# Channel shuffle on one core: three in-place slots of 68 KB in place of two input and three output buffers of 38 KB

## The chip, the cores and the metric

The kernel runs on one core of a Trainium2 chip. The metric is the device time of one execution in microseconds; the kernel before takes 316.18 us (median of 3 runs, 316.15 to 316.26). The profile comes from one execution and counts from its first instruction to its last.

## What is computed

The input is `[16, 64, 64, 256]` in fp32: 65,536 rows of 256 channels, 1 KB a row, 67.11 MB in all. In each row the 256 channels are read as 8 groups of 32 and written as 32 groups of 8:

```python
x = x.reshape(batch, h, w, groups, channels_per_group)   # 8 x 32
x = x.transpose(0, 1, 2, 4, 3)
x = x.reshape(batch, h, w, c)
```

There is no arithmetic. Every byte is loaded once and stored once, and each row is permuted inside itself.

## The kernel before, in words

A tile of q is q rows of 1 KB on each of the 128 partitions, so 128 q rows that lie together in HBM, q KB without a break for each partition. The list `_SLOTS` (line 12) cuts the 512 rows a partition into slots of one or two tiles: `[4, 8]`, `[28]`, twelve of `[38]`, and `[16]`, which makes sixteen tiles. The loop at line 45 goes over the slots. For each it takes an `in_tile` from a pool with two buffers and an `out_tile` from a pool with three (lines 36, 37, 46, 47), each buffer with room for 38 KB a partition, 190 KB a partition together.

For each tile three instructions are written down:

- line 55: SP issues the load, one DMA from HBM into the input buffer;
- line 57: VectorE (DVE) copies the tile from the input to the output buffer and permutes each row on the way, with a read pattern of step 32 inside the row and a dense write;
- line 61: ACT issues the store, one DMA from the output buffer to HBM.

`tc.manual_schedule` (line 43) keeps this order on each engine; the framework adds the waits. A load into an input buffer waits until the copy that read this buffer two slots earlier is done. A copy waits for its load and, through the output buffer, for the store of three slots earlier. A store waits for its copy. All loads go through SP's queue (q1 in the profile), all stores through ACT's (q10), each in order; the same 16 DMA engines serve both. PE and GpSimd do no work on the data.

Of the kernel before, what the change touches and what calls it, by code (L numbers as in the profile page):

```python
# [1 line left out]

# [4 lines left out]


F32 = mybir.dt.float32
P = 128  # L10

_SLOTS = [[4, 8], [28]] + [[38]] * 12 + [[16]]
_IN_BUFS = 2
_OUT_BUFS = 3


@with_exitstack
def kernel(
    ctx: ExitStack,
    tc: tile.TileContext,  # L20
    x: bass.AP,
    groups: bass.AP,
    out: bass.AP,
):
    nc = tc.nc
    b, h, w, c = x.shape
    G = int(groups)
    CPG = c // G
    assert G * CPG == c
    assert sum(map(sum, _SLOTS)) * P == b * h * w  # L30
    biggest = max(map(sum, _SLOTS))

    x_flat = x.rearrange("b h w c -> (b h w c)")
    out_flat = out.rearrange("b h w c -> (b h w c)")

    in_pool = ctx.enter_context(tc.tile_pool(name="in_pool", bufs=_IN_BUFS))
    out_pool = ctx.enter_context(tc.tile_pool(name="out_pool", bufs=_OUT_BUFS))

    def rows(flat, first, q):

        return flat[first * c : (first + P * q) * c].rearrange("(p f) -> p f", p=P)

    ctx.enter_context(tc.manual_schedule(engines=None))
    first = 0
    for parts in _SLOTS:
        in_tile = in_pool.tile([P, biggest * c], F32, name="in_tile")
        out_tile = out_pool.tile([P, biggest * c], F32, name="out_tile")
        at = 0
        pieces = []
        for q in parts:  # L50
            pieces.append((q, first, slice(at * c, (at + q) * c)))
            first += P * q
            at += q
        for q, start, cols in pieces:
            nc.sync.dma_start(out=in_tile[:, cols], in_=rows(x_flat, start, q))  # L55
        for q, start, cols in pieces:
            nc.vector.tensor_copy(  # L57
                out=out_tile[:, cols].rearrange("p (i j g) -> p i j g", j=CPG, g=G),
                in_=in_tile[:, cols].rearrange("p (i g j) -> p i j g", g=G, j=CPG),
            )  # L60
            nc.scalar.dma_start(
                out=rows(out_flat, start, q), in_=out_tile[:, cols]
            )


# [1 line left out]
_INS = ['x', 'groups']  # L67
_OUTS = [((16, 64, 64, 256), 'float32')]

_NUMBERS = {'groups': 8}  # L70


# [26 lines left out]
```

## Time and profile before

| | value |
|---|---|
| median of the runs | 316.18 us |
| span of the profiled execution | 314.4 us |
| what lies around the span (median less span) | 1.8 us |
| VectorE busy, 16 copies | 119.0 us, 38% of the span |
| loads, 16 DMAs | 67.11 MB |
| stores, 16 DMAs | 67.11 MB |
| median time from issue to landing, 38-KB tile | load 37.0 us, store 42.6 us |

The profiled execution's own time outside its span is not recorded; the table takes the median in its place, so that a change of the span is carried over to the time as it is.

How to read the page: part 2 cuts the span into 40 equal slices. The digits behind an engine are its busy share in tenths, those behind DMA the mean busy share of the 16 DMA engines, and GB/s is what they moved. A packet is booked in the slice in which it starts, so a single slice can lie above or below the true rate, and so can a short window. Part 3 gives the two queues with packets, bytes, and the share of the 16 engines' span that their packets took. A row of a tile on one partition goes as one packet here: 16 DMAs of 128 partitions and 16 closing packets of 4 B for each DMA are the 2,304 packets of a queue.

The trace also holds each DMA packet with its queue, size, start and duration. These are called the packet records below.

### The profile page before, as it was taken

How to read it: one execution, taken by the hardware profiler on the slowest of the kernel's cores; microseconds unless marked ns; L12 is line 12 of the kernel's file. 1: busy time of each engine (PE TensorE's matmuls, PEld its weight loads, DVE VectorE, ACT ScalarE, POOL GpSimd, SP SyncE). 2: the span in 40 equal slices, each digit the busy share in tenths (PEclk: the TensorE clock that was granted, in tenths of full speed). 3: DMA queues.
4: the chain of work that ended last, by engine and by line, in shares of the span. 5: the costliest groups of instructions: out<-in, count | busy, mean ns of one | idle time of the engine just before them, and what ended most of it. 6: DMA issues, size and time to landing. Idle time of an engine off the chain costs nothing.

```text
span 314.4 us, 132 instructions
## 1 busy us (share of the span) xinstructions
DVE 119.0 (38%) x16; POOL 0.2 (0%) x4
## 2 busy tenths in 40 slices
DVE  2081907309109109019028028037046055065400
POOL 0000000000000000000000000000000000000000
DMA  7999999999999999999999999999999999999997
GB/s 317 405 441 416 435 416 483 401 465 406 450 421 446 426 436 436 401 470 396 475 396 475 396 470 401 470 401 470 401 450 421 446 426 436 436 417 450 429 421 321
DMA packets 4608, 134.22 MB, mean 427 GB/s; under 512 B 512, under 2 KB 512, under 8 KB 768
## 3 DMA queue, kind: packets, MB, share of 16 engines
q1 hardware_dynamic: 2304, 67.11, 49.8%
q10 hardware_dynamic: 2304, 67.11, 49.4%
HBM read 67.11 MB, written 67.11 MB: 427 GB/s over the span
## 4 chain that ended last, share of the span: by engine, by line
DMA 76%; DVE 19%; issue 0%; SPq 0%; DVEq 0%
DMA in_tile<-in_x_dram 76%; DVE out_tile L57 19%; SPq L55 0%; DVEq L57 0%
## 5 line engine op out<-in xcount | busy, mean ns | idle before, releaser
L57 DVE COPY out_tile<-in_tile 128x9728 f32<-128x9728 f32 (+4 forms) x16 | 119.0, 7440 | 179.4 <-DMA in_tile<-in_x_dram 179.4
L80 POOL MEMSET const-uint8-127<- 128x1 uint8 x1 | 0.1, 103 | 0.0
L80 POOL MEMSET const-bfloat16-1.0<- 128x1 bf16 x1 | 0.1, 102 | 0.0
L80 POOL MEMSET const-float32-1.0<- 128x1 f32 x1 | 0.1, 100 | 0.0
L80 POOL MEMSET const-float32-0.0<- 128x1 f32 x1 | 0.1, 99 | 0.2 <-issue 0.2
## 6 DMA issues: line engine op xcount, KB each, us to landing
in_tile<-in_x_dram SPq DMA_DIRECT2D x12, 4864.0 KB, 37.0
out_dram<-out_tile ACTq DMA_DIRECT2D x12, 4864.0 KB, 42.6
in_tile<-in_x_dram SPq DMA_DIRECT2D x1, 3584.0 KB, 14.7
out_dram<-out_tile ACTq DMA_DIRECT2D x1, 3584.0 KB, 30.9
in_tile<-in_x_dram SPq DMA_DIRECT2D x1, 2048.0 KB, 30.4
out_dram<-out_tile ACTq DMA_DIRECT2D x1, 2048.0 KB, 15.2
in_tile<-in_x_dram SPq DMA_DIRECT2D x1, 1024.0 KB, 5.4
out_dram<-out_tile ACTq DMA_DIRECT2D x1, 1024.0 KB, 25.0
```

What stands on the lines that cost most here:

```text
L57: nc.vector.tensor_copy(out=out_tile[:, cols].rearrange("p (i j g) -> p i j g", j=CPG, g=G), in_=in_tile[:, cols].rearrange("p (i g j) -> ...
L80: nc = _bacc.Bacc("TRN2", target_bir_lowering=False, num_devices=1)
```

## The change

The two pools become one pool of three slots, each with room for 68 KB a partition (56 of the largest tile and 12 of `_SHIFT`), 204 KB together. The tiles are `[4, 8, 28]` in the first slot, then eight of `[56]`, then `[24]`: twelve tiles for sixteen.

A tile is loaded 12 KB further up in its slot than it is stored from. VectorE moves it down in place, in chunks of at most 12 rows: chunk by chunk, `src` is 12 KB above `dst`, so a chunk's source and destination touch but don't overlap, and each chunk is written where the one before it was read. A tile of 56 takes five copies (four of 12 rows, one of 8), one of 28 three, one of 24 two. The store of a tile still comes after all of its copies. A load into a slot now has to wait until the store that read this slot three slots earlier has landed, since the load writes over the bytes that it reads.

```diff
-_SLOTS = [[4, 8], [28]] + [[38]] * 12 + [[16]]
-_IN_BUFS = 2
-_OUT_BUFS = 3
+_SLOTS = [[4, 8, 28], [56]] + [[56]] * 7 + [[24]]
+_BUFS = 3
+_SHIFT = 12
...
-    biggest = max(map(sum, _SLOTS))
+    room = max(map(sum, _SLOTS)) + _SHIFT
...
-    in_pool = ctx.enter_context(tc.tile_pool(name="in_pool", bufs=_IN_BUFS))
-    out_pool = ctx.enter_context(tc.tile_pool(name="out_pool", bufs=_OUT_BUFS))
+    pool = ctx.enter_context(tc.tile_pool(name="pool", bufs=_BUFS))
...
-        in_tile = in_pool.tile([P, biggest * c], F32, name="in_tile")
-        out_tile = out_pool.tile([P, biggest * c], F32, name="out_tile")
+        slot = pool.tile([P, room * c], F32, name="slot")
...
-        for q, start, cols in pieces:
-            nc.sync.dma_start(out=in_tile[:, cols], in_=rows(x_flat, start, q))
-        for q, start, cols in pieces:
-            nc.vector.tensor_copy(
-                out=out_tile[:, cols].rearrange("p (i j g) -> p i j g", j=CPG, g=G),
-                in_=in_tile[:, cols].rearrange("p (i g j) -> p i j g", g=G, j=CPG),
+        for q, start, at in pieces:
+            nc.sync.dma_start(
+                out=slot[:, (at + _SHIFT) * c : (at + _SHIFT + q) * c],
+                in_=rows(x_flat, start, q),
             )
+        for q, start, at in pieces:
+            for lo in range(at, at + q, _SHIFT):
+                n = min(_SHIFT, at + q - lo)
+                src = slot[:, (lo + _SHIFT) * c : (lo + _SHIFT + n) * c]
+                dst = slot[:, lo * c : (lo + n) * c]
+                nc.vector.tensor_copy(
+                    out=dst.rearrange("p (i j g) -> p i j g", j=CPG, g=G),
+                    in_=src.rearrange("p (i g j) -> p i j g", g=G, j=CPG),
+                )
             nc.scalar.dma_start(
-                out=rows(out_flat, start, q), in_=out_tile[:, cols]
+                out=rows(out_flat, start, q), in_=slot[:, at * c : (at + q) * c]
             )
```

More of the change, by code (lines that the diff above doesn't have):

```diff
@@ L50 @@
         for q in parts:
-            pieces.append((q, first, slice(at * c, (at + q) * c)))
+            pieces.append((q, first, at))
             first += P * q
             at += q
-        for q, start, cols in pieces:
-            nc.sync.dma_start(out=in_tile[:, cols], in_=rows(x_flat, start, q))
-        for q, start, cols in pieces:
-            nc.vector.tensor_copy(
-                out=out_tile[:, cols].rearrange("p (i j g) -> p i j g", j=CPG, g=G),
-                in_=in_tile[:, cols].rearrange("p (i g j) -> p i j g", g=G, j=CPG),
-            )
+        for q, start, at in pieces:
+            nc.sync.dma_start(
+                out=slot[:, (at + _SHIFT) * c : (at + _SHIFT + q) * c],
+                in_=rows(x_flat, start, q),
+            )
+        for q, start, at in pieces:
[7 more added lines that the diff above has]
+                )
             nc.scalar.dma_start(
-                out=rows(out_flat, start, q), in_=out_tile[:, cols]
+                out=rows(out_flat, start, q), in_=slot[:, at * c : (at + q) * c]
             )
```

## The prediction

> **What bounds the kernel now.** I read the page first, parts 2 and 3:
>
> ```profile
> span 314.4 us, 132 instructions
> ...
> DMA  7999999999999999999999999999999999999997
> ...
> q1 hardware_dynamic: 2304, 67.11, 49.8%
> q10 hardware_dynamic: 2304, 67.11, 49.4%
> ```
>
> The two queues together fill the 16 DMA engines for 99.2% of the span, and only the first and last slice show a 7. The loads' packets took 0.4% of the span, 1.3 us, more than the stores' for the same bytes and count. Next the windows, one row for the middle (length, DVE busy, POOL busy, clock, DMA share, GB/s):
>
> ```profile
> 60.00:260.00 200.00, 75.15 (x9) 0.00 (x0) 1.00 1.00 433
> ```
>
> DMA share is 1.00. VectorE is busy for 75 of these 200 us. Part 4 gives it a share of the chain all the same:
>
> ```profile
> DMA 76%; DVE 19%; issue 0%; SPq 0%; DVEq 0%
> ```
>
> This is how the load of two tiles later is released (buffer free when the copy ends), not a limit: the DMA engines work on the other queue meanwhile. The timeline shows the beat:
>
> ```profile
> 71.31 8.75 DVE L57 COPY out_tile<-in_tile 128x9728 f32<-128x9728 f32 x1 [13.40 <-DMA in_tile<-in_x_dram]
> ...
> 94.33 8.77 DVE L57 COPY out_tile<-in_tile 128x9728 f32<-128x9728 f32 x1 [14.27 <-DMA in_tile<-in_x_dram]
> ...
> 278.19 8.73 DVE L57 COPY out_tile<-in_tile 128x9728 f32<-128x9728 f32 x1 [14.21 <-DMA in_tile<-in_x_dram]
> ```
>
> From 71.31 to 278.19 are nine beats, 22.99 us each, in which 38 rows go in and 38 out, and in each VectorE waits 14 us for a load. So the time is the DMA engines' work, and a gain can only come from what they do besides moving bytes.
>
> The packet records say how much that is. In the full stream, start to start on one engine, a packet of 4, 8, 16, 28 and 38 KB takes 0.1554, 0.3060, 0.6070, 1.0585 and 1.4353 us: 37.65 ns per KB and 4.7 ns per packet. A closing packet takes 5.9 ns. Check: a beat is 16 x 1.4353 + 2 x 0.006 = 22.98 us. One engine's 8,192 KB then cost 308.4 us, its 256 data packets 1.2 us, its 32 closing packets 0.2 us. The rest of the span is 1.75 us until the first packet, about 1.2 us after the last, and some 1.7 us ahead of 36 us and in the engines' uneven end. The records put 1.13 us of that on loads that take longer than their size asks, all before 36 us, when loads run nearly alone; behind it, no load does. Within rounding, this is the 1.3 us of part 3.
>
> **The change, part by part.**
>
> *Fewer, longer packets.* 24 DMAs for 32, 8 packets of each on an engine: 64 data packets less, 64 x 4.7 ns = 0.30 us, and 8 closing packets less, 0.05 us. Gain 0.35 us. A packet of 56 KB is not in the trace; by the two nearest rows (28 and 38 KB) it takes 56 x 0.03765 + 0.0047 = 2.113 us. Bounds: as above, or 1% longer, as loads ran around 20 us (third part).
>
> [...]
>
> *The in-place copies.* From the groups by form:
>
> ```profile
> L57 DVE COPY out_tile<-in_tile 128x4096 f32<-128x4096 f32 x1 | 3.9, 3873 | 7.6 <-DMA in_tile<-in_x_dram 7.6
> L57 DVE COPY out_tile<-in_tile 128x2048 f32<-128x2048 f32 x1 | 2.0, 2019 | 1.5 <-DMA in_tile<-in_x_dram 1.5
> L57 DVE COPY out_tile<-in_tile 128x1024 f32<-128x1024 f32 x1 | 1.1, 1092 | 4.1 <-DMA in_tile<-in_x_dram 4.1
> ```
>
> A chunk of 12 rows (3,072 elements) lies midway between 2,019 and 3,873 ns: 2.95 us. A tile of 56: 4 x 2.95 + 2.02 = 13.8 us, with about 0.05 us between copies 14.05 us. VectorE's sum grows from 119.0 to 1.09 + 2.02 + 6.98 + 8 x 13.8 + 5.9 = 126 us, far below the span. Whether a copy inside one slot runs at the pace of one between two buffers is not shown; between that pace and twice as long, I take the former, since elements, pattern and types are those of the rows above. The cost is nothing while it is hidden by the DMA queues; the cover is counted below.
>
> [...]
>
> *The load's new wait.* Load i+3 waits for store i to land, not for a copy. Behind it on SP stand only later loads. The records show how the queues share: packet by packet in turn, whatever the packets' sizes. So by hand:
> - Up to 15.8 us nothing differs (loads 4, 8, 28). Load 1 (56) then runs against two 4-KB and five 8-KB store packets and ends at about 34.6. Load 2 runs against two of 8 KB and five of 28 KB: 8 x 2.113 + 0.6 + 5.3, ends at about 57. Three more 28-KB packets: store 28 is through at about 61.
> - Load 3 now issues at 61.4 (a landing is seen 0.4 to 0.7 us after its last packet). Its packets enter 1.0 us later (before: issue 0.73, first packet 1.75) behind two or three store packets already taken (before: first store issued at 5.19, first packet at 9.2, two loads ahead). So near 67 us. Meanwhile store 1, issued at 34.6 + 0.6 + 14.05 = 49.3, fills the engines alone; stores alone run at full pace at the end of before. Cost 0.
> - Then pairs of 2 x 2.113: a load or store takes 33.8 us. Store 1 ends at 67 + 5 x 4.226 = 88.1, load 3 at 98.7, and so on: the slot for the next load is free some 10 us before it is its turn. Copy: when load n lands, store n-1 has about six of eight packets left, at pair pace over 20 us, against 0.6 + 14.05 + 1.4.
> - The tightest place is the end. The last packet of load 8 passes at 67 + 6 x 33.8 - 2.1 = 267.7. Six packets of store 7 (12.7 us) and load 9's eight of 24 KB (7.3 us) remain: work until 287.7. Store 8 can begin at 267.7 + 0.6 + 14.05 + 1.4 = 283.8. Slack 3.9 us. Then stores 8 and 9 run alone, as 38 and 16 do before. Cost 0.
>
> *The start.* Beyond 15.8 us the records hold 0.54 us of slow loads before: 0.18 spread over the first 38-KB load (1.3% of 13.6 us), and 0.36 in one packet on each engine at 32.9 us, for which I see no reason. After, loads run nearly alone until 43.8. At 1.3% (the 38-KB load, the nearest row) that is 0.36 us, at 3% (the 28-KB load, 0.26 of 8.5 us) 0.84. With or without the 0.36: 0 to 1.2 us in place of 0.54, so -0.54 to +0.66. By the nearest row it is 0.36 or 0.72; I take the middle: no change.
>
> *Sum*: 314.4 - 0.35 = 314.05 us of span; with 1.8 us around it (median less span) 315.83 us, 0.11% below the median. Its own range, by the start: 315.3 to 316.5.
>
> **The rivals.**
> 1. *The start goes well or the middle gains more*: the 0.36 and half of the spread vanish, or longer packets also hide other gaps: 315.0 to 315.5. For: the 0.36 came once only. Against: loads run alone for longer.
> 2. *Long rows slow the loads* (the other side). If 56-KB loads run 1.3% long not only at the start but beside stores too, 64 packets of 2.113 us cost 1.8 us more: 317.6 us. It decides from 0.7% (0.98 us: the 0.35 gained and 0.63 to the edge). For: the only packets that ran long are loads. Against: from 36 us on none did, at 38 and 16 KB.
> 3. *In-place copies are slow.* At 1.28 times the slack of 3.9 us is gone; at twice, 14 - 3.9 = 10 us idle before store 8: 326 us. For: such a copy is not in the trace. Against: the forms between two buffers lie close to one line from 4 to 38 rows.
> 4. *The change doesn't do what it says*: a 56-KB row goes as two packets. Then 64 + 64 more packets: 0.6 us on the forecast, 316.4, no difference.
>
> **How the numbers follow.** A measurement of this kernel can tell about 0.2%, 0.63 us, from no change, so the edges are 315.55 and 316.81. Main case 0.64, of which 0.21 falls below 315.55; rival 1, 0.09; rival 2, 0.15; rival 3, 0.08; rival 4, 0.04. Faster 0.21 + 0.09 = 0.30; same 0.43 + 0.04 = 0.47; slower 0.15 + 0.08 = 0.23. The range 315.0 to 317.2 leaves out rival 3 and two thirds of rival 2, 0.18.
>
> **What would show it.** Right: packets 2 x 1,728, DMA share 1.00 in the middle, VectorE near 126 us, copies of 3,072 elements near 2.95 us, landings 33.8 us apart, both queues' shares closer than 0.4%. Wrong: a slice below 9 near 61 or 285 us; a load queue's share above the store queue's by more than 0.6%; copies above 3.7 us; packets above 1,728 a queue.

## The result and the profile after

| | before | after |
|---|---|---|
| median (range, runs) | 316.17 us (316.15 to 316.26) | 317.89 us (317.50 to 318.38, 4) |
| span of the profiled execution | 314.4 us | 315.6 us |
| end of an engine's last packet, mean of the 16 engines | 312.97 us | 312.90 us |
| the same: first, median, last of the 16 engines | 312.86, 312.92, 313.28 us | 312.47, 312.75, 314.50 us |

The changed kernel is slower: 1.72 us, ratio 1.0056 [1.0042, 1.0070]. The forecast was 315.8 us, the range ended at 317.2. The profiled execution of the changed kernel took 317.50 us, the lower end of its times, so its trace shows 1.2 of the 1.72 us. All ratios here leave out executions that took over 1.5% longer than the fastest of their kernel, two of no_copy_56_3_slots and three of after_half_loads.

The lines of the page that answer to those of before:

```profile
span 315.6 us, 145 instructions
...
DVE 126.6 (40%) x47; POOL 0.2 (0%) x4
...
DMA  8999999999989999998999899989999998999986
...
DMA packets 3457, 134.22 MB, mean 425 GB/s; under 512 B 385, under 2 KB 385, under 8 KB 641
...
q1 hardware_dynamic: 1728, 67.11, 49.6%
q10 hardware_dynamic: 1728, 67.11, 49.1%
...
DMA 81%; DVE 13%; issue 0%; SPq 0%; DVEq 0%
```

The packets are the 1,728 of a queue that were foretold; the odd one, 3,457, is a packet of 24 B in the instruction queue at 0.2 us. Both queues' shares are lower; they stand 0.5 apart, between the 0.4 that the prediction set for right and the 0.6 for wrong. Scattered 8s are mostly booking: a 56-KB packet of 2.1 us counts in the slice where it starts, and none of them stands at 61 or 285 us, where the prediction looked for one. The middle by the windows (length, DVE busy, POOL busy, clock, DMA share, GB/s) is as full as before, and so is the rate, 435 GB/s for 433:

```profile
60.00:260.00 200.00, 82.86 (x30) 0.00 (x0) 1.00 1.00 435
```

The timeline shows the start of each tile's copies, and in the brackets how long VectorE had waited for the load:

```profile
59.84 13.96 DVE L64 COPY slot<-slot 128x3072 f32<-128x3072 f32 x5 [10.28 <-DMA slot<-in_x_dram]
99.86 14.01 DVE L64 COPY slot<-slot 128x3072 f32<-128x3072 f32 x5 [26.07 <-DMA slot<-in_x_dram]
133.74 13.96 DVE L64 COPY slot<-slot 128x3072 f32<-128x3072 f32 x5 [19.87 <-DMA slot<-in_x_dram]
...
269.54 13.93 DVE L64 COPY slot<-slot 128x3072 f32<-128x3072 f32 x5 [20.09 <-DMA slot<-in_x_dram]
294.15 5.91 DVE L64 COPY slot<-slot 128x3072 f32<-128x3072 f32 x2 [10.68 <-DMA slot<-in_x_dram]
```

Landings stand 33.9 us apart, a tile's copies take 14.0 us, and the last big tile's store is issued at 283.5 us: the beat, the copies and the cover at the end are those of the prediction.

So no average shows the loss. It is in the last microseconds, after (first fence) and before (second fence):

```profile
312.00:313.00 1.00, 0.00 (x0) 0.00 (x0) 1.00 0.29 123
313.00:314.00 1.00, 0.00 (x0) 0.00 (x0) 1.00 0.06 25
```

```profile
312.00:313.00 1.00, 0.00 (x0) 0.00 (x0) 1.00 0.65 279
313.00:314.00 1.00, 0.00 (x0) 0.00 (x0) 1.00 0.00 0
```

A DMA share of 0.06 is one engine of sixteen. Before, most engines are busy past 312 us and all stop together. After, most have stopped by then and one works on, to 314.50 us. The mean engine ends 0.07 us earlier, the median engine 0.17 us earlier, and the last one 1.22 us later: that is the growth of the span.

**Where the late engine lost it.** The packet records don't name the engine. I put a packet down to the engine whose packet before it ended as it began, which fits to a few ns behind 60 us. They give each packet's duration, and that of nearly all goes by the size alone: a typical 56-KB packet takes 2.113 us start to start, which is what 28 and 38 KB led to. Call a packet stalled when it takes over 15 ns more than its size asks. After 60 us, 1 of 1,328 load packets is stalled before (0.07 us in all), and 23 of 896 after (4.29 us, 0.02 to 0.50 us each). Stores hardly stall (2 of 1,168 after, 0.43 us). The late engine lost 1.64 us: seven of the stalled loads (1.21 us) and both stalled stores. Before, no engine is more than 0.36 us behind the median; after, the last one is 1.75 us behind it and 0.85 us behind the next. The whole time is set by that engine.

The late engine is also out of step with the others. Load 3 was issued at 62.0 us into an empty load queue. From 63.9 to 67.4 us 15 engines start their third 56-KB packet of store 1, and one, the late one, its first of load 3:

```profile
q10 hardware_dynamic: 15, 0.86, 56.7%
q1 hardware_dynamic: 1, 0.06, 3.8%
```

From then on it often loads while the others store. Between 60 and 260 us it moves data in the same direction as most engines in 52% of the time, each of the 15 others in 93% or more. Below, an engine is called out of step when this share is about a half or less.

### The profile page after: what moved, and what is told of

Same layout as the page of the kernel before. It is cut to its first block, busy times and chain, and to the rows that moved or that the text cites. A ratio compares the mean times of both kernels' runs of the same rounds, so it can differ in the third digit from the quotient of the medians.

```text
span 315.6 us, 145 instructions
## 1 busy us (share of the span) xinstructions
DVE 126.6 (40%) x47; POOL 0.2 (0%) x4
## 2 busy tenths in 40 slices
DMA packets 3457, 134.22 MB, mean 425 GB/s; under 512 B 385, under 2 KB 385, under 8 KB 641
## 3 DMA queue, kind: packets, MB, share of 16 engines
q1 hardware_dynamic: 1728, 67.11, 49.6%
q10 hardware_dynamic: 1728, 67.11, 49.1%
## 4 chain that ended last, share of the span: by engine, by line
DMA 81%; DVE 13%; issue 0%; SPq 0%; DVEq 0%
DMA out_dram<-slot 43%; DMA slot<-in_x_dram 39%; DVE slot L64 13%; SPq L55 0%; DVEq L64 0%
## 5 line engine op out<-in xcount | busy, mean ns | idle before, releaser
L64 DVE COPY slot<-slot 128x3072 f32<-128x3072 f32 (+2 forms) x47 | 126.6, 2694 | 173.4 <-DMA slot<-in_x_dram 172.2
## 6 DMA issues: line engine op xcount, KB each, us to landing
out_dram<-slot ACTq DMA_DIRECT2D x1, 3072.0 KB, 14.8
```

The source lines that it names most:

```text
L64: nc.vector.tensor_copy(out=dst.rearrange("p (i j g) -> p i j g", j=CPG, g=G), in_=src.rearrange("p (i g j) -> p i j g", g=G, j=CPG),)
```

## The experiments

Three things changed at once: rows of 56 KB for 38, copies inside a slot for copies between buffers, and loads that wait for a store to land. My theories of the stalls, by the names that the expectations use: SIZE, that long packets bring them; PLACE, that in-place copies do, by work on the memory beside the DMA engines; STEP, that the load queue runs dry once, near 61 us, and leaves engines out of step, which collect delays; LATE, that a load issued only a few packets ahead of its turn is served unevenly. PITCH (that rows 56 KB apart in HBM collide) and FETCH (the instruction packet) came up on the way. Each ratio is against the kernel before, run in the same batch, whose medians lay between 316.06 and 316.19 us.

**1. The changed kernel again**, with no edit.

> The changed kernel once more, unaltered, for its spread and for a second look at the packets. Three theories. STEP: the load queue runs dry once, from about 59 to 67 us, the 16 DMA engines take up load 3 at different packets, and an engine that is a packet out of step with the others collects delays; then the late engine shows again (some engine over 1 us behind the middle one at the end), and the time is 317.5 to 318.4. SIZE: packets of 56 KB make loads run long now and then beside stores; same time, but the late packets are spread over engines that are in step too. PLACE: copies inside the slot disturb the DMA to the same slot; same time, late packets fall in the copies' 14 us.

Measured: 318.89 us (316.69 to 320.72, 6 runs), 1.0084 [1.0052, 1.0115]. The profiled execution has 33 stalled loads (8.46 us). Its last engine ends at 315.46 us, 2.6 behind the median:

```profile
313.00:314.00 1.00, 0.00 (x0) 0.00 (x0) 1.00 0.17 74
314.00:315.00 1.00, 0.00 (x0) 0.00 (x0) 1.00 0.11 49
```

What follows: the loss is real, its size differs from run to run by 4 us, and again a few engines are late at the end. Here all 16 engines left the dry queue in step, so being out of step from there isn't needed for the loss.

**2 and 3. The tiles of before in the slots of after, and a start without the dry queue.**

```diff
-_SLOTS = [[4, 8, 28], [56]] + [[56]] * 7 + [[24]]
+_SLOTS = [[4, 8], [28]] + [[38]] * 12 + [[16]]        # same_tiles_3_slots
+_SLOTS = [[4], [36]] + [[56]] * 8 + [[24]]            # one_tile_head
```

> In place with three slots, but with the tiles of the kernel before (4 and 8, 28, twelve of 38, 16). STEP: by the queues' turns load 3 issues only after the 8 KB store, near 30 us, where load 2 has just ended: dry for a few us, so late engines are possible: 316.2 to 317.5. SIZE: no packet above 38 KB, so 316.2 within 0.3. PLACE: as the changed kernel, 317 or more.

> The changed kernel with the head 4, 36 in slots of their own in place of 4, 8, 28 in one slot; the eight tiles of 56 and the 24 stay. By the queues' turns load 3 issues at about 24 us and load 2 runs until 35, so the load queue never runs dry. STEP: no engine falls out of step, 315.8 (eight packets and a DMA fewer for each queue than the changed kernel, so down to 315.7). SIZE: 317.2 or more. PLACE: 317.2 or more.

Measured: 317.13 us (316.82 to 321.39, 12 runs), 1.0052 [1.0025, 1.0079]; and 318.88 us (317.94 to 319.19, 5), 1.0077 [1.0065, 1.0089]. The second has load 3 issued in time and is as slow as any: its stalls are 37 (6.43 us), and it is late at the end as well:

```profile
313.00:314.00 1.00, 0.00 (x0) 0.00 (x0) 1.00 0.35 147
314.00:315.00 1.00, 0.00 (x0) 0.00 (x0) 1.00 0.17 74
```

What follows: the dry queue near 61 us isn't needed. Being out of step is not ruled out, though: in one_tile_head five engines are out of step (35 to 49%, the others 87% or more), all 37 stalled loads are theirs, and they are the last five to end (314.46 to 315.49 us, the next at 313.39). The first run, in which one engine also lost 0.84 us to the instruction packet of experiment 4, says that 38-KB tiles don't cure it all, and raised PLACE and LATE.

**4 and 8. A fourth slot at 38 KB, then chunks of 13 rows.** With four slots the loads are issued some 18 us ahead of their turn (before: 14.8); the copies stay in place.

```diff
-_SLOTS = [[4, 8, 28], [56]] + [[56]] * 7 + [[24]]
-_BUFS = 3
+_SLOTS = [[4, 8], [28]] + [[38]] * 12 + [[16]]
+_BUFS = 4
```

In same_tiles_4_slots_13, `_SHIFT = 13` besides: 43 copies for 55.

> In place with four slots of 50 KB and the tiles of the kernel before. Loads issue about 20 us ahead of their turn, the queue never runs dry. STEP: 316.2 within 0.3, no late engine. SIZE: 316.2 within 0.3. PLACE: 317 or more, since the copies are in place here as well.

> In place with the permutation, tiles of the kernel before, four slots of 51 KB and a shift of 13 in place of 12: a tile of 38 takes three copies in place of four, 42 copies in place of 53. With a shift of 12 the one late engine of this kernel lost 0.84 us beside an 8 KB packet of the instruction queue at 268.7 us. FETCH (that packet is the cause): it falls out of the run, no engine is late, 316.2 within 0.2 in place of 316.7. PLACE (copies in the slot cost DMA time): stays at 316.7.

Measured: 316.70 us (316.65 to 316.83, 11 runs), 1.0014 [1.0005, 1.0023]; and 316.35 us (316.17 to 316.62, 11), 1.0003 [0.9995, 1.0012]. The profile of the first names what remains, in part 3:

```profile
span 314.9 us, 169 instructions
...
q14 instruction: 2, 0.01, 0.0%
```

One of these packets, 8 KB of instructions, comes at 268.66 us. On the engine that takes it there is a gap of 0.30 us and then the only stalled load of the run, 0.54 us: that engine is 0.84 us late. With 157 instructions in place of 169 no such packet comes between 268 and 292 us, and the run is like before: 0 stalls, last engine at 313.23 us.

What follows: PLACE falls, as in-place copies of 38-KB tiles cost nothing (1.0003 in same_tiles_4_slots_13); FETCH holds, and is worth about 0.35 us here (316.70 less 316.35). In the changed kernel (145 instructions) the packet came after the end, at 316.83 us, so FETCH is not its cause.

**5, 6 and 7. No copies at all.** The copy loop (from line 60) is taken out and `_SHIFT` is 0, so the permutation is left out and a slot is only loaded and stored.

```diff
+_SLOTS = [[8]] + [[56]] * 9            # no_copy_56_3_slots
+_SLOTS = [[8], [45]] + [[51]] * 9      # no_copy_51_3_slots; no_copy_51_4_slots with _BUFS = 4
```

> Leaves the permutation out: each tile is stored from where it was loaded, so VectorE does nothing and the slots need no 12 KB more. Tiles 8 and nine of 56, three slots of 56. By the queues' turns a load issues some five packets (about 10 us) ahead of its turn, against two to four in the changed kernel. From the packet count alone (96 data and 12 closing packets fewer on an engine) 315.65 us. PLACE (copies disturb the DMA): 315.6, no stalled packet after 60 us. SIZE (56 KB packets stall): over 316.5, stalled load packets as before. LATE (a load issued only a few packets ahead of its turn stalls engines): between the two.

> Permutation left out, tiles 8, 45 and nine of 51, three slots. A load issues about five packets ahead. From the packet count 315.75 us. LATE: stalls, 316.3 or more, and more than with four slots. SIZE: stalls, the same as with four slots. PLACE: none.

> The same with four slots: a load issues about thirteen packets (27 us) ahead of its turn. LATE: 315.75 us and no stalled packet. SIZE: the same stalls as with three slots. PLACE: none in either.

Measured: 317.94 us (316.66 to 322.2, 11 runs), 1.0051 [1.0030, 1.0072]; 317.32 us (316.75 to 317.86, 9), 1.0031 [1.0017, 1.0044]; 317.02 us (316.50 to 317.37, 11), 1.0024 [1.0015, 1.0033]. Stalled loads are 17, 9 and 6. The first packet of a load waits about 28, 23 and 55 us in its queue: these loads are issued long before their turn.

What follows: without VectorE and with loads issued early, rows of 51 and 56 KB still cost 0.24 to 0.51%. That speaks for SIZE, and against PLACE and LATE as conditions of it. It doesn't speak for SIZE alone: in no_copy_56_3_slots four engines are out of step (32 to 42%), all 17 stalled loads are theirs, and they end last.

**11, 13 and 14. Long rows with the buffers of before.** Two input and two output buffers, one copy per tile, as in the kernel before but for the tiles (and a third output buffer less, to make room).

```diff
-_OUT_BUFS = 3
+_OUT_BUFS = 2
 _SLOTS = [[4, 8], [28]] + [[38]] * 12 + [[16]]    # out_of_place_38, as before
+_SLOTS = [[4, 8], [28]] + [[44]] * 10 + [[32]]    # out_of_place_44
+_SLOTS = [[4, 8], [28]] + [[50]] * 9 + [[22]]     # out_of_place_50
```

> The kernel before with two output buffers and its own tiles. Loads issue about three packets of 38 KB ahead, in place of five. SIZE: 316.2 within 0.2, no stalled packet. LATE: 316.6 or more, stalls on the packets behind a change of DMA.

> The same with ten tiles of 44 and one of 32: the step between 38 (no stalled packet, 316.12 us) and 50. By the packet count 0.15 us less than before, 315.95. SIZE: between, 315.9 to 316.5; if it is a limit between 38 and 50 KB, either no stalled packet or as many as at 50.

> The kernel before with two output buffers and tiles 4 and 8, 28, nine of 50, 22, all even, since copies of an odd number of rows took twice as long (51 rows 22.3 us) and spoiled the run with 51. Out of place, one copy a tile, no dry queue by the turns, about 75 us of slack a tile less the copy of 11.5 us. By the packet count 0.24 us less than before: 315.9. SIZE (load packets of 50 KB stall now and then whatever the rest of the kernel): stalled packets after 60 us, 316.5 to 317.2. STEP or in place alone: none, 315.9.

Measured:

| rows | us (range, runs) | ratio | stalled loads after 60 us |
|---|---|---|---|
| 38 KB | 316.12 (316.01 to 316.44, 11) | 1.0001 [0.9992, 1.0010] | 0 of 1,328 |
| 44 KB | 316.35 (316.13 to 317.05, 11) | 1.0012 [1.0003, 1.0021] | 3 of 1,104, 0.10 us |
| 50 KB | 317.52 (316.24 to 318.06, 6) | 1.0040 [1.0027, 1.0054] | 13 of 992, 2.29 us |

The middle of the 38-KB and of the 50-KB kernel by the windows:

```profile
60.00:260.00 200.00, 73.56 (x9) 0.00 (x0) 1.00 1.00 433
```

```profile
60.00:260.00 200.00, 80.67 (x7) 0.00 (x0) 1.00 1.00 433
```

Both are full. The 50-KB profile fell on that kernel's fastest execution (316.24 us; the other five took 317.36 or more), so its stalls are seen in a run where they did not add up on one engine. In it no engine is out of step (84% or more): long load packets stall in step too.

What follows: this is the cleanest answer. Same copies, same kind of buffers, 30% longer rows: 1.4 us (317.52 less 316.12). SIZE is shown, as a cost in time and in stalls; that the stalls make up the whole 1.4 us is not, since no slow execution was traced. LATE falls as the cause here: at 38 KB a load is issued 9.1 us before its first packet and nothing is lost, at 50 KB 12.2 us before, and it stalls. At shorter leads (6 to 7 us in the changed kernel, 7 to 8 in three slots at 38 KB) it is not ruled out.

**10. Rows of 51 KB with the buffers of before**, meant for the same question.

```diff
-_OUT_BUFS = 3
+_OUT_BUFS = 2
+_SLOTS = [[4, 8], [28]] + [[51]] * 9 + [[13]]
```

> The kernel before with two output buffers in place of three and tiles 4 and 8, 28, nine of 51, 13: out of place, one copy a tile. By the packet count 0.24 us less than before, 315.9. With two output buffers a copy waits for the store two slots earlier, so that a load issues some three packets ahead of its turn, as in the changed kernel. SIZE: stalled packets after 60 us, 316.6 to 317.3. LATE: the same. PLACE or the in-place slots: 315.9.

Measured: 366.2 us (363.81 to 367.05, 5 runs), 1.1582 [1.1557, 1.1608]. The copies got in the way, but they are not all. By groups (busy us, mean ns of one), this kernel and then the one with 50 rows:

```profile
L57 DVE COPY out_tile<-in_tile 128x13056 f32<-128x13056 f32 x9 | 200.4, 22274 | 116.9 <-DMA out_dram<-out_tile 116.9
```

```profile
L57 DVE COPY out_tile<-in_tile 128x12800 f32<-128x12800 f32 x9 | 103.5, 11500 | 156.6 <-DMA out_dram<-out_tile 156.6
```

One row more, an odd number, and a copy takes 22.27 us for 11.50: half the pace on VectorE. But VectorE then waits some 14 us a tile for a store, and the DMA engines are hardly ever idle in the middle; they move less (the last column, GB/s):

```profile
60.00:260.00 200.00, 125.74 (x7) 0.00 (x0) 1.00 0.99 367
```

From 60 to 300 us a 51-KB packet takes 2.34 us as a load and 2.15 us as a store on average, for 1.93 us in no_copy_51_3_slots, and that while VectorE copies as well as while it waits. So the length doesn't settle a packet's time by itself. What made these packets long is open; it is the largest loss of all the runs.

**12 and 15. Three slots at 38 KB with larger slots.** After experiment 4 the slower three slots of experiment 2 were open. `_SHIFT` 19 and then 20 move the slots apart, make two copies a tile, and remove the instruction packet inside the run.

```diff
-_SHIFT = 12
+_SHIFT = 19    # same_tiles_3_slots_19
+_SHIFT = 20    # same_tiles_3_slots_20
```

(with the tiles of experiment 2)

> In place, three slots, the tiles of the kernel before, shift 19 in place of 12: two copies a tile, so that the instruction queue's 8 KB packet, which came at 290 us in the run with shift 12 (317.13 us), falls out. SIZE and FETCH: 316.3 within 0.3. LATE or STEP (three slots alone bring late engines): 316.6 or more, with engines over 0.5 us behind at the end.

> In place, three slots, tiles of the kernel before, shift 20: two copies a tile of 20 and 18 rows, both even, few enough that no packet of the instruction queue falls inside the run. The same run with shift 12 had that packet (0.84 us on one engine) and another engine 1.1 us behind by stalled 38 KB packets. SIZE alone: 316.2 within 0.3. STEP (the load queue is dry near 30 us and an engine that comes out a packet apart stalls even at 38 KB): 316.5 to 317.2, the late engine being one that is a packet apart from the others.

Measured: 320.81 us (320.51 to 321.51, 4 runs), 1.0151 [1.0137, 1.0165]; and 317.11 us (316.18 to 318.15, 8), 1.0035 [1.0022, 1.0047]. The first is spoiled by the same thing, as the groups show (first the kernel with 19, then with 20):

```profile
L64 DVE COPY slot<-slot 128x4864 f32<-128x4864 f32 x25 | 210.2, 8407 | 78.3 <-DMA slot<-in_x_dram 77.9
```

```profile
L64 DVE COPY slot<-slot 128x5120 f32<-128x5120 f32 x13 | 62.2, 4788 | 170.4 <-DMA slot<-in_x_dram 170.4
```

With 19 rows the copies take 16.85 us a tile, and most DMA engines stand idle for about 4.7 us before 302 us, until the last store may start. The second is free of that and of the instruction packet and still costs 0.35%: 8 stalled loads (1.94 us), 17 stalled stores (4.94 us, most near 296.6 us).

What follows: three slots cost something at 38 KB too (1.0035), where four cost nothing (1.0003). In same_tiles_3_slots_20 it looks like what its expectation calls STEP: the load queue is dry near 30 us, two engines come out of it a packet apart from the others (near 35 us) and stay out of step (24 and 28%, the others 88% or more). All 8 stalled loads are theirs, and they end last, at 314.38 and 314.68 us, the next at 313.70. This is seen in one profile and not tested by a run of its own. Why 17 stores stall I can't say; of the profiles read here only out_of_place_51 has more time in stalled stores behind 60 us.

**9, 16 and 17. The changed kernel with 56-KB tiles moved as two DMAs of 28 KB**: both directions, only the loads, only the stores.

```diff
+    def halves(q):
+
+        return [(0, q // 2), (q // 2, q)] if q == 56 else [(0, q)]
...
-            nc.sync.dma_start(
-                out=slot[:, (at + _SHIFT) * c : (at + _SHIFT + q) * c],
-                in_=rows(x_flat, start, q),
-            )
+            for a, z in halves(q):
+                nc.sync.dma_start(
+                    out=slot[:, (at + _SHIFT + a) * c : (at + _SHIFT + z) * c],
+                    in_=rows(x_flat, start, q)[:, a * c : z * c],
+                )
```

(the store alike)

> The changed kernel, unaltered but that each load and store of a 56 KB tile is issued as two DMAs of 28 KB a partition, so that no packet is longer than 28 KB; slots, waits, copies and row addresses stay. By the packet count 128 data and 16 closing packets more on an engine than the changed kernel, 0.7 us: 316.5 us if no engine is late. SIZE (long packets stall): 316.5 within 0.3 and hardly a stalled packet after 60 us. LATE (loads issued a few packets ahead of their turn): in packets the lead doubles, so fewer stalls too, but the place of the slots' wait in time is the same. PITCH (rows 56 KB apart in HBM collide): stays at 318.

> The changed kernel with only the loads of the 56 KB tiles issued as two DMAs of 28 KB a partition; stores keep packets of 56 KB. By the packet count 0.35 us more than the changed kernel's own sum, 316.2. If it is the length of the load packet that makes it stall: no stalled load after 60 us, 316.2 within 0.4. If it is the length of the store packets beside it: stalls as in the changed kernel, 317.5 or more. The queues' turns go packet by packet, so the stores now get two thirds of the time while both queues are full, and the store queue runs dry instead of the load queue.

> The same with only the stores halved; load packets stay at 56 KB and get two thirds of the time while both queues are full, so the load queue waits for slots. Load length: stalled loads as in the changed kernel, 317.5 or more. Store length: none, 316.2 within 0.4.

Measured: both halved, 317.43 us (317.26 to 317.54, 5 runs), 1.0041 [1.0028, 1.0053]; with halved loads 317.68 to 317.89 us in three runs, 1.0051 [1.0033, 1.0069], and 328 to 333 us in three more, the profiled one among them, so that its trace is not used; with halved stores 318.38 us (318.06 to 320.02, 5), 1.0080 [1.0061, 1.0100].

With both halved, everything else of the change stays and the stalls go: 1 of 1,773 loads, and that one follows the instruction packet, which came at 289.66 us here. Three engines are out of step in this run as well (24 to 31%), without a stall. The page:

```profile
span 315.7 us, 182 instructions
...
q1 hardware_dynamic: 2880, 67.11, 49.8%
q10 hardware_dynamic: 2880, 67.11, 49.3%
q14 instruction: 1, 0.01, 0.0%
```

The time is hardly better, since the cure has prices of its own: 1,152 more packets a queue, by the prediction's terms about 0.7 us an engine; the instruction packet on one engine, 0.84 us; a start slower by 0.4 us than before. The engines end between 313.39 and 314.43 us, all of them later than before. With stores alone halved the loads stall as ever (39 of 896, 5.33 us) and one engine ends 3.6 us behind the median.

What follows: with the slots, waits, copies and row addresses of the change kept, packets of 28 KB in both directions do not stall (1 of 1,773 loads), in step or out of it. So here it takes packets longer than 28 KB, and PITCH falls, as a cause of the stalls. This is shown in the records, not in the time.

## Why the prediction was wrong

- **"Fewer, longer packets"** is the step that failed. Its price is right for packets that don't stall: a typical 56-KB packet takes the predicted 2.113 us, so that an engine's packets come to 0.35 us less. Its two bounds, as above or 1% longer, were bounds on a uniform cost. What came is not uniform: behind 60 us 23 of 896 load packets stall, 4.29 us in all, and one engine lost 1.64 us, its stalled stores included. On the mean engine the stalled loads cost 0.27 us and the start 0.15 us more than before, so it ends only 0.07 us earlier; the last one, which sets the time, ends 1.22 us later. In the records of before, the engines' ends lay within 0.42 us, and the sum took it for granted that they would stay so.
- **"The in-place copies"**: right. 2,951 ns for a chunk (2.95 priced), 126.6 us in all (126), and no cost: four slots with 38-KB tiles give 1.0003.
- **"The load's new wait"**: its times are right. Store 28 was through at 61.4 us (61), load 3 issued at 62.0 us (61.4), landings 33.9 us apart (33.8), the last big store issued at 283.5 us (283.8). The slack of 3.9 us held. "Cost 0" for the dry queue is not shown to be right: load 3 was to come "behind two or three store packets", and it came behind two on one engine and three on 15. The sum put this difference at nothing, and that one engine ended last. In after_again the loss came without it, so how much of the 1.72 us it brings is open.
- **"The start"**: loads slower than their size before 60 us cost 1.28 us an engine for 1.13, so +0.15 us within -0.54 to +0.66. Right.
- **Rival 2, "long rows slow the loads"**, had the side and, by luck, the size: 1.8 us priced, 1.72 measured. Its form was wrong: it let every load packet run 1.3% long, where 97% of them run exactly as predicted. The test that I set for it, load share above store share by more than 0.6%, shows 0.5% and would have missed it. It got 0.15 because beside stores hardly a load ran long at 38 KB (1 stalled, by 0.07 us); no row of before held a longer packet, so that argument reached further than its rows.
- **Rivals 1, 3 and 4** did not come: 317.9 us, copies at full pace, packets of 1,728.

Fewer and larger DMAs did not pay here: eight DMAs less brought the mean engine 0.07 us and the kernel a loss of 1.72 us, and out_of_place_50, with fewer and larger DMAs than out_of_place_38, is slower by 1.4 us.

**What stays open.** Why a long load packet stalls at all. In the changed kernel 15 of the 23 stalls (3.06 us) stand directly behind a load packet that has only a store's closing packet between, with no store data; 112 load packets stand so, and of the 784 others 8 stall. At 50 KB it is 9 of 13, in 128 such places; at 38 KB (out_of_place_38) there are 160 such places and no stall. So the place matters together with the length, and nothing here shows by what. Being out of step goes with stalls too. In four profiles (after, one_tile_head, no_copy_56_3_slots, same_tiles_3_slots_20) engines are out of step from 66 us or earlier; in each of them these end last, and in three of them all stalled loads are theirs. No run changes that alone, so it is seen, not shown as a cause; an engine can also fall out of step by its delays, as the last one of same_tiles_3_slots did (45%). Also open: how the changed kernel's 0.56% divides between the length, the engine out of step and the three slots, and what made the packets of out_of_place_51 long. Four slots of 68 KB would take 272 KB a partition and were not tried.

None of the versions beats the kernel before; out_of_place_38 and same_tiles_4_slots_13 equal it.

## What to carry to other kernels

Here the DMA share was 1.00 from 60 to 260 us in both kernels, and the span grew with the end of the last of the 16 engines (313.28 to 314.50 us), while their mean end (312.97 to 312.90 us) and the rate (433 to 435 GB/s) improved. So compare where each engine's last packet ends: shares and rates are means. Per-packet cost was 0.4% of this kernel's span (1.2 of 314.4 us); to save a part of it, rows of 44 KB lost 0.12% and rows of 50 KB 0.40%, where the packet counts had promised 0.05 and 0.08% less. Cost an operation whose size lies beyond every row of the profile by bounds that allow for rare, uneven delays, not by a uniform per cent alone.

## What the runs showed of the hardware that was not expected

- **Copies of an odd number of rows took nearly twice as long as their size asks.** Chunks of 13 and of 12 rows in one kernel (same_tiles_4_slots_13; busy us, mean ns):

```profile
L64 DVE COPY slot<-slot 128x3328 f32<-128x3328 f32 x27 | 156.8, 5806 | 98.3 <-DMA slot<-in_x_dram 97.9
L64 DVE COPY slot<-slot 128x3072 f32<-128x3072 f32 x12 | 35.5, 2960 | 0.4
```

  5,806 ns for 2,960, though 13 rows are 8% more; 51 rows for 50 (22,274 ns for 11,500) and 19 for 20 (8,407 for 4,788) show the like. Every odd row count that ran (3, 9, 13, 19, 51) did so (9 rows took 4,064 ns in the kernel with 19, where 8 took 2,018); what makes it so, the traces don't show.
- **An 8-KB packet of instructions made one DMA engine 0.84 us late**: a gap of 0.30 us and a load packet longer by 0.53 us, alike in three runs (same_tiles_4_slots, same_tiles_3_slots, after_half_rows), at 268.66, 290.03 and 289.66 us. With twelve instructions fewer than same_tiles_4_slots (same_tiles_4_slots_13) none came between 268 and 292 us.
